# Decoder trunk on one core: the last projection and gate with tokens on partitions, two output products per feature tile in two matmuls, the first key weights in single tiles, and another table of steps

## The chip, the core and the metric

One core of a Trainium2 chip runs the whole program in one launch. The metric is the device time of one execution in microseconds (us), lower is better. TensorE (PE in the profile) multiplies matrices out of SBUF into PSUM, whose space is eight banks of 128 partitions by 512 float32; VectorE (DVE) and ScalarE (ACT) do the elementwise work; GpSimd (POOL) does a few small powers; SyncE (SP) issues nearly all DMAs.

## What is computed

Two layers on a residual stream `x` of 256 tokens by 1024 features, float32. The first mixes tokens by block-sparse attention (with 256 tokens: plain causal attention), the second by three gated branches (compressed, selected and sliding-window attention). After each mixer a per-layer embedding `p` is projected, gated and added:

```python
for i in range(DEPTH):                                  # DEPTH = 2
    h = rms_norm(x, norm_gain[i])
    x = x + (moba_layer if i % 2 == 0 else nsa_layer)(h, ...)     # q, k, v, z = h @ w_in; attention; silu(z); @ w_out
    gate = jax.nn.sigmoid(rms_norm(x, ple_gate_gain[i]) @ ple_w_gate[i])
    x = x + gate * (p[i] @ ple_w_proj[i])
return x                                                # (1, 256, 1024)
```

Here `w_out` and `ple_w_gate` are 1024 by 1024, and `ple_w_proj` is 256 by 1024.

## The kernel before

**Layout.** `x` lies in SBUF as `xT`, features on partitions: eight tiles ("k" 0 to 7) of 128 features by 256 tokens. Every float32 product is made of float32r ones: an operand is split into a high part (rounded by ACT) and a low part (the remainder, by DVE), and high x high, high x low and low x high are added in PSUM. Of a weight the parts are `hi` and `lo` (cut from `raw` or, when small, from a `tmp` buffer, where the DMA put it); of an activation they are `ah` and `al`, two tiles of 128x256. There are five `raw`, five `hi` and five `lo` buffers, and five `tmp`.

**Units.** A projection of 512 output features is a `Unit` (line 510). `mul` (529) makes its products for one k. With `feat` the features come out on partitions: the weights are stationary and the 256 tokens stream, so a tile of 128 output features takes three products of 256 columns. Without `feat` the tokens come out on partitions: an activation tile of 128 tokens is stationary and 512 weight columns stream, three products of 512 columns for each half of the tokens. q, k and v are of the second sort; z, `w_out` (steps `o0`, `o1`, in layer 1 `no0`, `no1`), the projection of `p` (`p0`, `np0`, ...) and the gate (`g0`, `ng0`, ...) of the first.

**The end of a layer** is `tail` (693). Step `x.k` gates an attention tile and splits it, `o` multiplies by `w_out`, `o>j` adds the result to `xT` (`add_out`, 723), `y.k` splits `xT` times a gain, `b` makes the norm: squares of `xT` summed in `sqacc`, two small products with `ones` into a `tr` bank, a power on POOL, two transposes that spread the result, `bc`. `g` multiplies, and `gate` (729) multiplies by `bc`, takes a tanh on ACT, multiplies by the projected `p` and adds to `xT`. In the last layer the output is stored from `xT`, feature-major, and the host transposes it.

**What sets the order.** Each step only records its operations. `PROGRAM` (line 25) is a table of steps whose order says which operation goes first when several are ready; a planner (`schedule`, 258) with costs of its own puts all operations of all engines into one order from it, and assigns the buffers. The table was found by a search. The first weights of q (`c0` to `c7`) are loaded as single tiles of one k, those of k (`k.0` to `k.3`) as pairs.

**Banks.** PSUM has the tags `mm` (four banks), `s` (two, scores) and `tr` (two, transposes and attention outputs). One line of the program (L394) issues every instruction, so the profile is read by tile names.

Of the kernel before, what the change touches and what calls it, by code (L numbers as in the profile page):

```python
# [24 lines left out]
PROGRAM = ("x0 w:c0 x2 c0 x1 w:c1 c1 x3 w:c2 c2 x4 w:c3 w:c4 x5 c3 w:c5 w:k.0 x6 w:c6 consts x7 k.0 w:c7 c4 w:k.1 c5 "  # L25
# [22 lines left out]

BEHIND = "k.0 k.2"
# [366 lines left out]
def trunk(ctx: ExitStack, tc: tile.TileContext, a, out):  # L416
# [79 lines left out]
    def split_act(src, gain=None, either=False):  # L496
        hi = apool.tile([P, T], F32R, tag="ah", name="ah")
        lo = apool.tile([P, T], F32R, tag="al", name="al")
# [9 lines left out]
        return hi, lo  # L508

    class Unit:  # L510
# [4 lines left out]
        def __init__(self, src, feat, xs, n=512, nk=KT, kg=2, apart=False, close=None):  # L515
            self.src, self.feat, self.xs, self.n, self.nk, self.kg, self.apart = src, feat, xs, n, nk, kg, apart
            self.ps, self.w, self.granules = None, {}, nk // kg
            self.whole = self.granules if close is None else close
            self.parts = [] if close is None else \
                [(b, (m,)) for b in range(2) for m in range(2)] if apart else [(0, (0, 1)), (1, (0, 1))]  # L520

        def weights(self, g):
            if self.ps is None:
                self.ps = [bank("mm", 4) for _ in range(2)]
                if self.apart:
# [3 lines left out]
        def mul(self, w, j, k, b, ms=(0, 1), cols=None, parts=(0, 1, 2)):  # L529
            (wh, wl), (xh, xl) = w, self.xs[k]  # L530
            first, last = k == 0, k == self.nk - 1
            if self.feat:
# [160 lines left out]
    def tail(i, oT, pvs, zin, xz, norm, after):  # L693
# [35 lines left out]
        def gate(u, j, m, n):  # L729
# [704 lines left out]
```

## Time and profile before

| | us |
|---|---|
| time, median of 3 runs | 361.81 (361.71 to 362.15) |
| time of the profiled execution | 362.87 |
| span of that execution, first to last instruction | 361.1 |
| TensorE busy in it | 354.9 (98%), 2569 matmul records |
| VectorE busy | 324.3 (90%) |
| ScalarE busy | 270.7 (75%) |
| main DMA queue, share of the 16 engines' span | 46.8% |

The profiled execution is 1.06 us above the median, and 1.8 us of it lie outside the span. The share of busy time of TensorE is the union of matmul records whose ends are modelled; successive matmuls overlap in them, so how fast it really goes is seen in the distance between starts. A name such as `mm<-ah,hi` is output, then inputs; the shape behind it is the moving operand's.

### The profile page before, as it was taken

The numbers are of one execution on the slowest core, as the hardware profiler recorded it, in microseconds if no ns is written. First come the engines' busy times: TensorE is split into PE (matmuls) and PEld (weight loads), VectorE is DVE, ScalarE is ACT, GpSimd is POOL, SyncE is SP. The second block draws the span as 40 slices with busy tenths as digits, with TensorE's granted clock in tenths as the row PEclk, the third lists the DMA queues.
The fourth block names the chain that finished last, engine by engine and source line by source line (L and its number), as shares of the span: only waits on it lengthen the run. The fifth ranks groups of instructions, "written<-read, shape, count | busy, mean of one in ns | idle before, by whom it ended". The sixth has DMA issues, their size and how long they took to land.

```text
span 361.1 us, 7132 instructions
## 1 busy us (share of the span) xinstructions
PE 354.9 (98%) x2569; PEld 322.3 (89%) x2569; DVE 324.3 (90%) x799; ACT 270.7 (75%) x592; POOL 29.0 (8%) x26
## 2 busy tenths in 40 slices
PE   8999999999999999999999999999999999999994
PEld 7688888888999999999889999767998999999994
DVE  5899999999999975969999999989999999967965
ACT  5667599986999854947665699969978989956711
POOL 1024104210000000000003300003000000000010
PEclk9999999999999999999999999999999999999998
DMA  7988456533554352745643534177363342142102
GB/s 223 364 315 273 160 195 230 176 118 99 178 190 148 114 181 74 227 165 176 204 136 115 211 120 172 60 285 287 129 246 134 120 130 104 57 157 80 59 31 87
DMA packets 20051, 58.97 MB, mean 163 GB/s; under 512 B 2480, under 2 KB 5296, under 8 KB 20016
## 3 DMA queue, kind: packets, MB, share of 16 engines
q1 hardware_dynamic: 19440, 58.04, 46.8%
q10 hardware_dynamic: 576, 0.48, 0.4%
q8 instruction: 20, 0.33, 0.4%
q14 instruction: 15, 0.12, 0.1%
HBM read 57.46 MB, written 1.05 MB: 162 GB/s over the span
## 4 chain that ended last, share of the span: by engine, by line
PE 92%; DVE 3%; ACT 2%; DMA 2%; issue 1%; SPq 0%; DVEq 0%; ACTq 0%
PE mm L394 71%; PE tr L394 12%; PE s L394 9%; DMA tmp<-in_p 2%; DVE lo L394 1%; DVE sm L394 1%; DVE tmp L394 1%; ACT sm L394 0%; ACT pt L394 0%; ACT tmp L394 0%; ACT hl L394 0%; ACT hi L394 0%; DVE c L394 0%; ACT big L394 0%; DVE kcB L394 0%
## 5 line engine op out<-in xcount | busy, mean ns | idle before, releaser
L394 ACT ACTIVATE hi<-raw 128x1024 fp32r<-128x1024 f32 (+2 forms) x100 | 99.0, 1006 | 29.9 <-PE mm L394 21.9
L394 DVE TENSOR_TENSOR lo<-raw,hi 128x1024 fp32r<-128x1024 f32 (+2 forms) x100 | 115.1, 1159 | 5.9 <-ACT hi L394 5.0
L394 PE MATMUL mm<-al,hi 128*128 128x256 f32 x416 | 116.9, 287 | 0.0
L394 PE MATMUL mm<-ah,lo 128*128 128x256 f32 x416 | 114.5, 286 | 0.0
L394 PE MATMUL mm<-ah,hi 128*128 128x256 f32 x416 | 114.2, 286 | 0.0
L394 PEld LDWEIGHTS mm<-al,hi 128*128 128x128 f32 x416 | 79.3, 191 | 0.2
L394 PEld LDWEIGHTS mm<-ah,lo 128*128 128x128 f32 x416 | 78.0, 191 | 0.3
L394 PEld LDWEIGHTS mm<-ah,hi 128*128 128x128 f32 x416 | 77.8, 191 | 0.4 <-issue 0.2
L394 PE MATMUL mm<-hi,ah 128*128 128x512 f32 (+2 forms) x178 | 67.5, 384 | 0.3 <-ACT hi L394 0.3
L394 PE MATMUL mm<-hi,al 128*128 128x512 f32 (+2 forms) x178 | 66.6, 377 | 0.0
L394 PE MATMUL mm<-lo,ah 128*128 128x512 f32 (+2 forms) x178 | 64.0, 377 | 0.0
L394 ACT ACTIVATE sm<-sm,nb 128x128 f32<-128x128 f32 (+1 forms) x96 | 42.6, 446 | 6.6 <-DVE nb L394 6.4
L394 PEld LDWEIGHTS mm<-hi,ah 128*128 128x128 f32 x178 | 33.9, 192 | 6.9 <-ACT hi L394 1.7
L394 PEld LDWEIGHTS mm<-hi,al 128*128 128x128 f32 x178 | 34.0, 192 | 5.1
L394 PEld LDWEIGHTS mm<-lo,ah 128*128 128x128 f32 x178 | 33.6, 191 | 5.2
L394 DVE CUSTOM_DVE_ANT_0 sm<-s,cst,nr_q 128x128 f32<-128x128 f32 (+1 forms) x96 | 36.2, 409 | 1.6 <-PE s L394 1.3
L394 ACT ACTIVATE pt<-tr 128x384 f32<-128x384 f32 x48 | 21.6, 482 | 3.9 <-PE tr L394 3.6
L394 PE MATMUL tr<-cst,sm 128*128 128x128 f32 x144 | 23.9, 274 | 0.2 <-ACT big L394 0.2
L394 POOL TENSOR_TENSOR r_q<-r,neg_half 128x16 f32<-128x16 f32 x5 | 15.8, 3150 | 77.0 <-DVE r L394 77.0
L394 ACT ACTIVATE tmp<-tmp 128x512 f32<-128x512 f32 (+3 forms) x22 | 11.2, 517 | 13.6 <-DVE tmp L394 13.5
L394 PEld LDWEIGHTS tr<-cst,sm 128*128 128x128 f32 x144 | 17.1, 140 | 2.3 <-DVE q L394 0.4
L394 ACT ACTIVATE ah<-xT,gain_in 128x256 fp32r<-128x256 f32 x31 | 14.8, 500 | 5.2 <-DVE xT L394 3.7
(176 smaller groups left out, 535.3 us busy)
## 6 DMA issues: line engine op xcount, KB each, us to landing
raw<-in_moba_in SPq DMA_DIRECT2D x28, 512.0 KB, 4.3
raw<-in_nsa_in SPq DMA_DIRECT2D x24, 512.0 KB, 3.5
raw<-in_w_out SPq DMA_DIRECT2D x16, 512.0 KB, 3.5
raw<-in_ple_gate SPq DMA_DIRECT2D x16, 512.0 KB, 3.9
raw<-in_w SPq DMA_DIRECT2D x8, 512.0 KB, 4.2
raw<-in_ple_proj SPq DMA_DIRECT2D x4, 512.0 KB, 3.8
raw<-in_nsa_vs SPq DMA_DIRECT2D x4, 304.0 KB, 2.8
xT<-in_x SPq DMA_DIRECT2D x8, 128.0 KB, 3.6
```

The lines of the kernel that those rows point to most:

```text
L394: getattr(getattr(self.nc, o.engine), o.method)(*[real(x) for x in o.args], **{k: real(x) for k, x in o.kwargs.items()})
```

## The change

1. **Fused pairs.** `split_act` puts both parts of an activation side by side in one tile of 128x512 (`both`; its names in built rows begin with `a_`). Where a unit is `wide`, each feature tile gets a PSUM bank of its own, and `mul` makes two products for it and a k instead of three: high weight by 512 columns (high and low activations at once, into the two halves of the bank) and low weight by 256 columns into the first half. The halves are added when they are taken out. `wide` are `w_out` of layer 1 (`no`) and the gate of layer 0 (`g`); half 0 of each takes all four `mm` banks, half 1 both `s` and both `tr`.
2. **Tokens on partitions** in the projection of `p` and the gate of layer 1. The gate then needs the norm as a number per partition (`rms`), which `square_x` takes on ACT from four transposed tiles at a time, and `xT` itself transposed: `turn_x` makes 16 transposes into `s` and `tr` banks. `gate_tok` runs tanh straight from PSUM with the norm as its scale, multiplies, adds and stores; the two norm products, the two transposes for `bc` and the multiplications by `bc` are gone from this layer. The output is stored token-major. The last part of the gate has 256 columns, and its end is done in two pieces of 128.
3. **Single key tiles.** The first four k of the keys' weights come as single tiles (`w:d0` to `w:d3`, products `d0` to `d3`) through `tmp` buffers.
4. **Another table `PROGRAM`**, so that most instructions stand elsewhere.

```diff
-PROGRAM = ("x0 w:c0 x2 c0 x1 w:c1 c1 x3 w:c2 c2 x4 w:c3 w:c4 x5 c3 w:c5 w:k.0 x6 w:c6 consts x7 k.0 w:c7 c4 w:k.1 c5 "
+PROGRAM = ("x0 w:c0 x1 w:c1 c0 w:d1 d0 x2 w:c2 x4 w:d2 x7 d1 x5 d2 x3 w:c3 w:d3 w:c4 w:c5 x6 consts a.1 a.3 w:c6 "
...
+WIDE = ('no', 'g')
+LAST = 1
+STORES = 4
...
     def split_act(src, gain=None, either=False):
-        hi = apool.tile([P, T], F32R, tag="ah", name="ah")
-        lo = apool.tile([P, T], F32R, tag="al", name="al")
+        both = apool.tile([P, 2 * T], F32R, tag="a2", name="a2")
+        hi, lo = both[:, :T], both[:, T:]
...
-        return hi, lo
+        return hi, lo, both
...
+            if self.wide:
+                for m in ms:
+                    o, s = self.ps[2 * b + m], slice((2 * b + m) * P, (2 * b + m + 1) * P)
+                    steps = [(o, wh[:, j, s], both)]
+                    steps.insert(0 if last else 1, (o[:, :T], wl[:, j, s], xh))
+                    for i, (d, y, x) in enumerate(steps):
+                        nc.tensor.matmul(d, y, x, start=first and i == 0, stop=last and i == len(steps) - 1,
+                                         skip_group_check=True)
+            elif self.feat:
...
+    MM, OTHER = (("mm", 4),) * 4, (("s", 2),) * 2 + (("tr", 2),) * 2
...
+        def add_out(u, j, m):
+            if u.wide:
+                for part in (slice(0, T), slice(T, 2 * T)):
+                    nc.vector.tensor_tensor(xT[:, m], xT[:, m], u.ps[j][:, part], op=OP.add)
...
+            if u.wide:
+                nc.scalar.activation(gr[:, 0], ps[:, T:], AF.Copy)
+                nc.vector.tensor_tensor(gr[:, 0], gr[:, 0], ps[:, :T], op=OP.add)
+                ps = gr.rearrange("p a b -> p (a b)")
...
+        def turn_x(h, t):
+            xps[h, t] = bank(*(("tr", 2) if h else ("s", 2)))
+            for k in range(4):
+                nc.tensor.transpose(xps[h, t][:, k * P:k * P + P], xT[:, 4 * h + k, t * P:t * P + P], ident)
...
+        def square_x(h, t):
+            nc.scalar.activation(tmp("sq"), xps[h, t], AF.Square, accum_out=sums[:, h, t:t + 1])
...
+        def gate_tok(u, j, h):
...
+                nc.scalar.activation(th, u.ps[t][:, a:b], AF.Tanh, scale=rms[:, t:t + 1])
+                nc.vector.scalar_tensor_tensor(y, th, 1.0, y, op0=OP.add, op1=OP.mult)
+                nc.vector.tensor_tensor(y, y, xps[h, t][:, a:b], op=OP.add)
...
-            u = Unit(a["ple_proj"][i, h], True, px, nk=2).steps(f"{n}p{h}")
+            u = Unit(a["ple_proj"][i, h], i == 0, px, nk=2).steps(f"{n}p{h}")
...
+                u = Unit(a["ple_gate"][i, h], False, xg, close=LAST if h else 2)
+                if h:
+                    u.parts = [(0, {}), (1, dict(cols=(0, 256))), (1, dict(cols=(256, 512)))]
```

Where instructions move. TensorE right after the products of k 1 for q (banks `mm_78`, `mm_79` are q's two halves of the tokens, in the new rows `mm_80` and `mm_81` are the keys'). Before:

```order
L394 MATMUL mm_79<-lo_130,ah_107 128x512
L394 MATMUL mm_78<-hi_126,ah_106 128x512
L394 MATMUL mm_78<-hi_126,al_115 128x512
L394 MATMUL mm_79<-hi_126,ah_106 128x512
L394 MATMUL mm_79<-hi_126,al_115 128x512
L394 MATMUL mm_78<-lo_131,ah_106 128x512
```

With the change:

```order
L399 MATMUL mm_79<-lo_125,a_1_110 128x512
L399 MATMUL mm_80<-hi_122,a_0_109 128x512 x2
L399 MATMUL mm_81<-hi_122,a_0_109 128x512 x2
L399 MATMUL mm_80<-lo_127,a_0_109 128x512
L399 MATMUL mm_81<-lo_127,a_0_109 128x512
L399 MATMUL mm_80<-hi_121,a_1_110 128x512 x2
L399 MATMUL mm_80<-lo_126,a_1_110 128x512
L399 MATMUL mm_81<-hi_121,a_1_110 128x512 x2
L399 MATMUL mm_81<-lo_126,a_1_110 128x512
L399 MATMUL mm_78<-hi_118,a_2_111 128x512 x2
```

Twelve key products on the first two x tiles now stand between q's second and third tile.

VectorE in layer 1, from the last piece of attention (`pcL`) to the first additions of `w_out` (`xT<-xT,mm`); `big<-big` gates the last attention tiles. Before:

```order
L394 TENSOR_TENSOR pcL_99<-tr_75,pcT_196 64x256
L394 TENSOR_TENSOR lo_131<-raw_136,hi_126 128x1024
L394 TENSOR_TENSOR lo_128<-raw_133,hi_123 128x1024
L394 SCALAR_TENSOR_TENSOR big_90<-big_89,big_90 128x256 x2
L394 TENSOR_TENSOR al_119<-big_90,ah_110 128x256
L394 TENSOR_TENSOR al_122<-big_90,ah_106 128x256
L394 TENSOR_TENSOR xT_63<-xT_63,mm_79 128x512
L394 TENSOR_TENSOR xT_63<-xT_63,mm_80 128x512
```

With the change:

```order
L399 TENSOR_TENSOR lo_124<-raw_128,hi_118 128x1024
L399 TENSOR_TENSOR lo_123<-raw_129,hi_120 128x1024
L399 TENSOR_TENSOR pcL_99<-tr_76,pcT_187 64x256
L399 TENSOR_TENSOR lo_127<-raw_130,hi_122 128x1024
L399 SCALAR_TENSOR_TENSOR big_88<-big_89,tr_75 128x512
L399 TENSOR_TENSOR a_5_114<-big_88,a_5_114 128x256
L399 TENSOR_TENSOR a_3_112<-big_88,a_3_112 128x256
L399 TENSOR_TENSOR xT_63<-xT_63,mm_80 128x256
L399 TENSOR_TENSOR lo_125<-raw_131,hi_119 128x1024
L399 TENSOR_TENSOR xT_63<-xT_63,mm_78 128x256
L399 TENSOR_TENSOR xT_63<-xT_63,mm_80 128x256
```

The last tiles are gated straight out of the bank, a weight split has moved in front of the additions and one between them, and each addition takes one half of a bank.

VectorE at the end of the program. Before:

```order
L394 TENSOR_TENSOR tmp_84<-s_165,bc_144 128x256
L394 TENSOR_TENSOR xT_63<-xT_63,tmp_85 128x512
L394 SCALAR_TENSOR_TENSOR tmp_83<-tmp_83,big_88 128x256
L394 TENSOR_TENSOR xT_63<-xT_63,tmp_83 128x256
L394 TENSOR_TENSOR tmp_86<-s_166,bc_144 128x128 x2
L394 SCALAR_TENSOR_TENSOR tmp_82<-tmp_82,big_88 128x128 x2
L394 TENSOR_TENSOR xT_63<-xT_63,tmp_82 128x128 x2
```

With the change:

```order
L399 SCALAR_TENSOR_TENSOR big_90<-tmp_83,big_90 128x512
L399 TENSOR_TENSOR big_90<-big_90,tr_75 128x512
L399 SCALAR_TENSOR_TENSOR big_90<-tmp_84,big_90 128x128
L399 SCALAR_TENSOR_TENSOR big_90<-tmp_85,big_90 128x128
L399 TENSOR_TENSOR big_90<-big_90,tr_76 128x128 x2
```

The multiplications by `bc` ahead of the last tanh are gone; a whole part of 512 columns now stands just ahead of the last pieces.

## Rows read from the trace of the kernel before

**Rows 1.** The page: span, TensorE's share, the chain that ended last by engine.

```profile
span 361.1 us, 7132 instructions
PE 354.9 (98%) x2569; PEld 322.3 (89%) x2569; DVE 324.3 (90%) x799; ACT 270.7 (75%) x592; POOL 29.0 (8%) x26
...
PE 92%; DVE 3%; ACT 2%; DMA 2%; issue 1%; SPq 0%; DVEq 0%; ACTq 0%
```

**Rows 2.** Timeline, TensorE: start us, us, instruction; 512 columns, then 256 columns.

```profile
20.25 0.39 PE L394 MATMUL mm<-lo,ah 128*128 128x512 f32 x1
...
21.39 0.39 PE L394 MATMUL mm<-hi,ah 128*128 128x512 f32 x1
...
344.24 0.28 PE L394 MATMUL mm<-ah,hi 128*128 128x256 f32 x1
...
345.80 0.28 PE L394 MATMUL mm<-al,hi 128*128 128x256 f32 x1
```

**Rows 3.** TensorE's timeline: norm products, transposes; one product left out of each.

```profile
341.76 0.50 PE L394 MATMUL tr<-ones,sqacc 128*128 128x2 f32 x4
...
342.32 0.28 PE L394 MATMUL mm<-ah,lo 128*128 128x256 f32 x1
...
346.52 0.38 PE L394 MATMUL tr<-cst,rstd 128*128 128x128 f32 x2
...
346.86 0.29 PE L394 MATMUL mm<-ah,lo 128*128 128x256 f32 x1
```

**Rows 4.** Timeline, TensorE (PEld: weight loads): a block of attention-times-value products.

```profile
320.47 0.28 PE L394 MATMUL mm<-ah,lo 128*128 128x256 f32 x1
...
320.68 2.82 PE L394 MATMUL tr<-pt,v 128*64 128x256 f32 x32
...
323.43 0.19 PEld L394 LDWEIGHTS tr<-pcT,vcB 128*128 128x128 f32 x1 [0.17 <-issue]
```

**Rows 5.** Busy by stretch (PE, PEld, DVE, ACT, ...); timelines at the start.

```profile
7.00:17.00 10.00, 9.73 (x39) 6.78 (x39) 8.48 (x16) 7.58 (x15) 0.00 (x0) 1.00 0.97 333
...
8.35 0.39 PE L394 MATMUL mm<-hi,ah 128*128 128x512 f32 x1
...
10.32 0.63 ACT L394 ACTIVATE hi<-raw 128x512 fp32r<-128x512 f32 x1 [1.25 <-DMA raw<-in_moba_in]
11.57 0.51 ACT L394 ACTIVATE ah<-xT,gain_in 128x256 fp32r<-128x256 f32 x1 [0.62 <-DMA xT<-in_x]
```

**Rows 6.** VectorE around layer 1's `w_out`; a group (busy, mean ns | idle).

```profile
321.54 2.36 DVE L394 TENSOR_TENSOR lo<-raw,hi 128x1024 fp32r<-128x1024 f32 x2 [1.82 <-ACT hi L394]
324.84 0.76 DVE L394 SCALAR_TENSOR_TENSOR big<-big,big 128x256 f32<-128x256 f32 x2 [0.94 <-ACT big L394]
...
328.28 0.69 DVE L394 TENSOR_TENSOR xT<-xT,mm 128x512 f32<-128x512 f32 x1 [1.77 <-PE mm L394]
329.48 0.69 DVE L394 TENSOR_TENSOR xT<-xT,mm 128x512 f32<-128x512 f32 x1 [0.51 <-PE mm L394]
...
L394 DVE TENSOR_TENSOR xT<-xT,tmp 128x256 f32<-128x256 f32 x7 | 2.8, 419 | 0.0
```

**Rows 7.** The end: timelines of three engines, a group of ScalarE.

```profile
356.22 0.28 PE L394 MATMUL s<-ah,lo 128*128 128x256 f32 x1
...
356.54 0.49 DVE L394 TENSOR_TENSOR tmp<-s,bc 128x128 f32<-128x128 f32 x2 [0.21 <-PE s L394]
...
356.92 0.51 ACT L394 ACTIVATE tmp<-tmp 128x128 f32<-128x128 f32 x2 [1.51 <-DVE tmp L394]
...
357.26 0.49 DVE L394 SCALAR_TENSOR_TENSOR tmp<-tmp,big 128x128 f32<-128x128 f32 x2 [0.24 <-ACT tmp L394]
357.67 0.49 DVE L394 TENSOR_TENSOR xT<-xT,tmp 128x128 f32<-128x128 f32 x2
...
358.19 0.36 ACTq L394 DMA_DIRECT2D out<-xT  x1
...
L394 ACT ACTIVATE v<-mm,rstd 128x256 f32<-128x256 f32 x4 | 1.8, 473 | 0.0
```

More of the change, by code (lines that the diff above doesn't have):

```diff
@@ L518, in __init__ @@
             self.whole = self.granules if close is None else close
             self.parts = [] if close is None else \
-                [(b, (m,)) for b in range(2) for m in range(2)] if apart else [(0, (0, 1)), (1, (0, 1))]
+                [(b, dict(ms=(m,))) for b in range(2) for m in range(2)] if apart else [(0, {}), (1, {})]
         def weights(self, g):
             if self.ps is None:
-                self.ps = [bank("mm", 4) for _ in range(2)]
-                if self.apart:
+                self.ps = [bank(*b) for b in self.wide or (("mm", 4),) * 2]
@@ L526, in weights, with mul @@
+                if self.apart and not self.wide:
                     self.ps = [ps[:, :T] for ps in self.ps + [bank("s", 2) for _ in range(2)]]
             self.w[g] = split(self.src[g], (self.kg, self.n))
-        def mul(self, w, j, k, b, ms=(0, 1), cols=None, parts=(0, 1, 2)):
-            (wh, wl), (xh, xl) = w, self.xs[k]
+        def mul(self, w, j, k, b, ms=(0, 1), cols=None, parts=(0, 1, 2), only=False):
+            (wh, wl), (xh, xl, both) = w, self.xs[k]
             first, last = k == 0, k == self.nk - 1
-            if self.feat:
+            if self.wide:
[7 more added lines that the diff above has]
+            elif self.feat:
@@ L541, in mul @@
                 c0, c1 = cols or (0, self.n)
+                w0, w1 = (c0, c1) if only else (0, c1 - c0)
                 o, s = self.ps[b][:, c0:c1], slice(b * P, b * P + P)
@@ L544, in mul @@
                     x, y = ((xh, wh), (xl, wh), (xh, wl))[i]
-                    nc.tensor.matmul(o, x[:, s], y[:, j], start=first and c0 == i == 0, stop=last and i == 2,
+                    nc.tensor.matmul(o, x[:, s], y[:, j, w0:w1], start=first and c0 == i == 0, stop=last and i == 2,
                                      skip_group_check=True)
@@ L746, in gate @@
-            if not last:
-                for k in range(m, m + n):
-                    after(k)
+            if u.wide:
+                nc.scalar.activation(gr[:, 0], ps[:, T:], AF.Copy)
+                nc.vector.tensor_tensor(gr[:, 0], gr[:, 0], ps[:, :T], op=OP.add)
+                ps = gr.rearrange("p a b -> p (a b)")
+            nc.vector.tensor_tensor(gr, ps.rearrange("p (a b) -> p a b", a=n),
+                                    n1.bc[:, None, :].to_broadcast([P, n, T]), op=OP.mult)
@@ new lines, in gate_tok @@
+        def gate_tok(u, j, h):
+            t, only = u.parts[j]
+            c0, c1 = only.get("cols") or (0, 512)
+            last = h == 1 and j == len(u.parts) - 1
+            for a, b in ((c0, c0 + P), (c0 + P, c1)) if last else ((c0, c1),):
+                th, y = tmp("th")[:, :b - a], pt[:, t, 512 * h + a:512 * h + b]
+                nc.scalar.activation(th, u.ps[t][:, a:b], AF.Tanh, scale=rms[:, t:t + 1])
+                nc.vector.scalar_tensor_tensor(y, th, 1.0, y, op0=OP.add, op1=OP.mult)
+                nc.vector.tensor_tensor(y, y, xps[h, t][:, a:b], op=OP.add)
+                for c in range(a, b, 512 // STORES if not h else 512):
+                    d = min(b, c + 512 // STORES) if not h else b
+                    (nc.scalar if last and a > c0 else nc.sync).dma_start(
+                        out[t, :, 512 * h + c:512 * h + d], pt[:, t, 512 * h + c:512 * h + d])
@@ L769, in tail @@
             todo[f"{n}y.{k}"] = lambda k=k: split_g(k)
-        n1.steps(f"{n}b")
+        if i:
+            todo[f"{n}b"] = norm_x
+        else:
+            n1.steps(f"{n}b")
     def pairs_pv(o, pairs):
@@ L810, in trunk @@
         o.after.append(i)
-    pair = [None]
+    pair = {}
     lows = {}
@@ L825, in first_w @@
             return
+        low = lows[k]
         c0, raw = 512 * (k % 2), second if k == 1 else None
         if k >= 4:
-            if not c0:
-                pair[0] = wpool.tile([P, 1024], F32, tag="raw", name="raw", bufs=NRAW)
-            raw = pair[0][:, c0:c0 + 512]
+            if k // 2 not in pair:
+                pair[k // 2] = wpool.tile([P, 1024], F32, tag="raw", name="raw", bufs=NRAW)
+            raw = pair[k // 2][:, c0:c0 + 512]
             nc.sync.dma_start(raw, a["moba_in"][0, k // 2, :, c0:c0 + 512])
@@ L860, in __init__ @@
                       "q": Unit(a["moba_in"][1], False, x0).steps("1q") if h else uq0}
+            if not h:
+                u = self.u["k"]
+                for k in range(4):
+                    todo[f"w:d{k}"], todo[f"d{k}"] = (lambda k=k: self.single(u, k)), (lambda k=k: self.tile(u, k))
+                for g in range(2):
+                    del todo[f"w:k.{g}"], todo[f"k.{g}"]
             for step in ("qe", "ke", "q", "k", "v"):
@@ L863, in __init__, with single, tile @@
             todo[n + "q+"], todo[n + "k+"] = (lambda: self.q2()), (lambda: self.k2())
+        def single(self, u, k):
+            if u.ps is None:
+                u.ps = [bank("mm", 4) for _ in range(2)]
+            u.w[f"d{k}"] = split(a["moba_in"][2, k // 2, :, 512 * (k % 2):512 * (k % 2) + 512], (1, 512), small=True)
+        def tile(self, u, k):
+            for b in range(2):
+                u.mul(u.w[f"d{k}"], 0, k, b)
         def qe(self):
@@ L985, in trunk @@
         todo[f"next.{k}"] = lambda k=k: next_x(k)
-    tail(0, oT, pvs, [a["moba_in"][6 + h] for h in range(2)], x0, n0, lambda k: None)
+    tail(0, oT, pvs, [a["moba_in"][6 + h] for h in range(2)], x0, n0)
     pe = consts.tile([P, 2, 16], F32, name="pe")
@@ L1314, in trunk @@
                 KD0=lambda: KD(0), KD1=lambda: KD(1))
-    tail(1, oT, pvs1, [a["nsa_in"][4 + h] for h in range(2)], x1, n2, lambda k: nc.sync.dma_start(out[:, k], xT[:, k]))
+    tail(1, oT, pvs1, [a["nsa_in"][4 + h] for h in range(2)], x1, n2)
     def run(step):
@@ L1432 @@
     got = r.results[0]["out_0"]
-    return _np.ascontiguousarray(got.transpose(1, 0, 2).reshape(D, T).T)[None]
+    return _np.ascontiguousarray(got.reshape(T, D))[None]
```

76 lines of the change are left out of this document (44 added, 32 removed), and 43 rows, old and new, of the table PROGRAM.

## The prediction

> **What bounds the kernel now.** First the page: of a span of 361.1 us TensorE is busy for 354.9, and the chain that ended last is TensorE for 92% [rows 1]. So the time is what TensorE needs for its list of products, plus the few places where it waits, plus the end behind its last product. How long it needs is not the mean of a matmul record, since records overlap: it is the distance between starts. In the timeline five steps of 512-column products take 1.14 us, 0.228 each, and thirteen steps of 256 columns take 1.56, 0.120 each [rows 2]. Twice 0.120 is more than 0.228: a product costs its columns and about 13 ns besides (0.240 less 0.228, by a step of 0.427 ns a column). That small difference is what most of the change lives on, for it leaves the number of columns as it is.
>
> TensorE waits in few places. Between 7 and 17 us it makes 39 products of 512 columns, 8.9 us of work in 10 [rows 5]; behind that the records leave next to nothing open. Its last product starts at 356.22, and the span ends 4.9 us later [rows 1, 7]. VectorE is busy 90% [rows 1], close to being the next bound, so each edit is also weighed there.
>
> **Fused pairs and tokens on partitions.** Counted in the built programs, products of 256 columns go from 1484 to 1024, those of 512 from 458 to 688. It comes out by hand: 128 pairs of a feature tile and a k are fused (64 each in `w_out` of layer 1 and the gate of layer 0), and of the three 256s of each two become one 512, -256 and +128 in all; the projection of `p` and the gate of layer 1 give up 48 + 192 of 256 for 102 of 512 and 36 of 256 (the last part is cut in two). Together -460 and +230, the same columns. By the paces: 460 x 0.120 = 55.2 less 230 x 0.228 = 52.4, so **-2.8 us**, all of it on the path, since TensorE is the path.
>
> The Trainium skill ("TensorE: Matmul & The Clock Gate", section "Wait — 56ns, not 53.3ns?") gives a warm matmul about 2.5 ns beyond its columns. By that figure the sum would lose most of this term: an estimate from it is 230 x 2.5 ns = 0.6 us. The rows disagree, with 13 ns a product, and they decide.
>
> **Added to TensorE.** 16 transposes of `xT`, less the two that spread the norm. Two transposes with one 256-column product among them take 0.34 us from 346.52 to 346.86 [rows 3], so 0.11 each: 14 x 0.11 = **+1.5 us**. The norm products of layer 1 go: four records with one product among them take 0.56, less 0.12 [rows 3]: **-0.4 us**. The new order has nine blocks of attention-value or compression products with a half-filled array, one more than before; a block costs its entry (0.21 to the next start for 0.12) and the 0.17 at its exit [rows 4], together 0.26: **+0.3 us**. TensorE in all: -2.8 + 1.5 - 0.4 + 0.3 = -1.4.
>
> **The start.** TensorE loses 10 - 39 x 0.228 = 1.1 us there, because weights and x tiles arrive late: the split at 10.32 had waited 1.25 us for its DMA, and that at 11.57 0.62 [rows 5]. With the change the keys' products `d0` and `d1` need only the first two x tiles and stand behind `c1`: 12 more products, 2.7 us, from about 8.35, where the third tile of q begins now [rows 5], to 11.1. Then `c2` is wanted. In SP's new order six x tiles and five weight tiles lead up to it, 6 x 128 + 5 x 256 = 2048 KB. The x split that waited until 11.57 had the same 2048 KB ahead of it and with it (x tiles 0 to 5 in its order of loading, `c0` to `c4`). So at worst `c2` is there at 11.5 and split at 12.1 (0.63 for a hi half [rows 5]): a wait of 1.0, and nothing gained. At best it comes earlier, as the transfers behind that x tile no longer share the engines, and all 1.1 goes. I take the middle, **-0.5**, bounds -1.1 and 0.
>
> **The join from attention to `w_out` of layer 1.** This is where VectorE gets more. Four additions of 512 (0.69 each) become 16 of 256 (0.42 each) [rows 6]: 6.7 - 2.8 = +3.9 us, and one weight split (2.36 for two) moves in front of the additions: +1.2. Against it, VectorE idles there for 1.82 + 0.94 + 1.77 + 0.51 = 5.0 us [rows 6]. So it goes from idle to just full. What hides it: between the first product on the last attention tile and the first gate product on tile 7 of the eight, TensorE has 22 products of 512, 24 of 256, then 16 transposes and 45 of 512, 67 x 0.228 + 24 x 0.12 + 16 x 0.11 = 19.9 us. VectorE owes in that time 16 additions (6.7), eight splits (0.48, 3.8 in all) and some five weight splits (1.2, 6.0): 16.5. It is covered, with 3.4 us to spare in sum, less at single places. I cost it at 0. If the cover fails: only the 1.77 + 0.51 of idle lies between additions, where more of them can go, so 5.1 - 2.3 = 2.8 is the most that TensorE could wait. The straight gating out of the bank (one operation of 512 in place of a copy and two of 256) shortens the same chain a little; I leave it out.
>
> **The gate of layer 0** gets a copy on ACT and an addition on VectorE for each of eight tiles, 8 x 0.42 = 3.4 us. Behind its last product the new order has 49 products of 512 of the next layer, 11.2 us, before the last x tile is used, and the chain of one tile is about nine operations of 0.4 to 0.5: hidden, 0. Without cover it would be one copy and one addition, 0.8.
>
> **The end.** Now: last product 356.22, multiplication by `bc` at 356.54, tanh at 356.92, two more operations, store issued at 358.19 [rows 7]. With the change tanh starts where the multiplication did; a tanh of 128 columns from PSUM with a scale is bounded by 0.47 for 256 [rows 7] and by the 0.3 that the present ones take apart. The first hop of 0.38 goes, up to 0.2 comes back in two slower tanhs: **-0.25**, bounds -0.5 and +0.1 (a part of 512 columns is finished just ahead on VectorE, and may be late).
>
> **Sum**: -1.4 - 0.5 - 0.25 = -2.15. The profiled execution took 362.87, so 360.7 for one like it; against the median, 361.81 - 2.15 = **359.7 us**.
>
> **The rivals.**
> *More waits go.* The whole 1.1 at the start (another -0.6), the end at -0.5, the extra block free (-0.3): 358.5. For it: all are bounds from rows. Against it: c2's 2048 KB.
> *The join turns into a wait.* VectorE comes late to the additions of `w_out`, the transposes of `xT` and the splits for the gate wait for it, and TensorE for them. Half of the 2.8 gives 361.1, about level with before. All of it, with nothing gained at the start, gives 359.7 + 2.8 + 0.5 = 363.0, **slower than before**. It decides at a wait of 2.1 us. For it: VectorE full where it idled. Against it: 3.4 us to spare.
> *The pairs don't do what they say.* Weights have to be loaded for each product; if in a 512 + 256 pair that shows, and a pair costs as three 256s, the 2.8 is gone: 359.7 + 2.8 = 362.5. For it: mixed runs of the two widths are few in the trace. Against it: 256-column products, each with a load of its own, keep 0.12. With the 0.6 that the skill's figure leaves (2.5 ns a product), it would be 361.9; as a mechanism here it means that the 0.12 is held up by something other than the product, and the even thirteen steps [rows 2] speak against it.
>
> **How the numbers follow.** Chances: forecast 0.55, more waits go 0.17, the join at half 0.11, the join in full 0.10, the pairs 0.05, the 2.5 ns 0.02. A measurement of this kernel tells about 0.2% from no change, 0.7 us: faster is below 361.1, slower above 362.5. Faster takes the forecast, the first rival and half of the join at half: 0.77; the rest of that, the 2.5 ns and half of the pairs are the same: 0.11; slower 0.12. The forecast's own range is 358.9 to 360.6 (start and end at their bounds, the join's first 0.3). The range over the cases, 358.0 to 361.9, leaves out some 0.06 below and 0.13 above.
>
> **What would show it.** Between steady starts 0.228 and 0.120 in the fused runs; last product near 354 in the span; one gap of up to 1 us on TensorE near 11 to 12 us, ended by ACT or VectorE's split of `c2`, and none behind it; at the end tanh directly behind the last product. Wrong would be: a wait of TensorE on VectorE between the last attention block and the gate of layer 1; pairs at over 0.36; or gaps in stretches that I have not looked at, since nearly every instruction moves.

## The result, and the profile after

The changed kernel takes 364.43 us (364.25 to 365.1, six runs); the kernel before, beside it, 361.98 (361.54 to 362.9, six runs). The ratio is 1.0072, 95% interval 1.0059 to 1.0086: **slower by 2.45 us**, where 2.15 less had been forecast. The profiled execution of after took 364.85, that of before 362.87.

The page of after (busy us, share of the span, instructions; then the chain that ended last by engine and by line) answers to [rows 1]:

```profile
span 362.7 us, 6746 instructions
...
PE 355.0 (98%) x2349; PEld 311.6 (86%) x2349; DVE 324.2 (89%) x806; ACT 274.4 (76%) x607; POOL 26.1 (7%) x26
...
PE 91%; DMA 5%; DVE 3%; ACT 1%; issue 0%; ACTq 0%; DVEq 0%
```

TensorE has 220 records less than before, and VectorE is no busier. But in the chain the share of DMA went from 2% to 5%. It is the first thing to follow. What TensorE waited for in after (us in total, times, longest):

```profile
PE mm L399 <- DVE hi L399: 1.4, 1, 1.4
PE tr L399 <- DVE ones L399: 1.1, 1, 1.1
PE s L399 <- DVE hl L399: 0.8, 1, 0.8
PE mm L399 <- ACT hi L399: 0.3, 1, 0.3
PE s L399 <- DVE nb L399: 0.2, 1, 0.2
```

and in before:

```profile
PE tr L394 <- DVE ones L394: 1.1, 1, 1.1
PE mm L394 <- ACT hi L394: 0.3, 1, 0.3
PE tr L394 <- ACT big L394: 0.2, 1, 0.2
```

The 1.1 at `ones` is the program's first microsecond and stands in both. New are 1.4, 0.8 and 0.2: two places stand out, and neither wait is at a product that was edited. A start delayed by a wait loses more than the idle shown here (1.5 for the 1.4, 0.9 for the 0.8, by the distance between starts), since the record ahead of it is drawn to its modelled end.

**The start** answers to [rows 5]. SyncE's issues and what hung on them in after (start, us, engine, instruction; in brackets the idle before it and what ended it):

```profile
1.63 0.43 SPq L399 DMA_DIRECT2D xT<-in_x  x1
2.10 0.91 SPq L399 DMA_DIRECT2D tmp<-in_moba_in  x2
...
6.96 0.51 ACT L399 ACTIVATE a<-xT,gain_in 128x256 fp32r<-128x256 f32 x1 [2.56 <-DMA xT<-in_x]
...
8.28 1.16 PE L399 MATMUL mm<-hi,a 128*128 128x512 f32 x4 [1.37 <-DVE hi L399]
...
15.73 0.50 PE L399 MATMUL mm<-hi,a 128*128 128x512 f32 x1 [0.25 <-ACT hi L399]
...
7.00:17.00 10.00, 8.47 (x36) 6.45 (x36) 8.21 (x16) 7.03 (x14) 0.00 (x0) 1.00 0.94 298
```

The chain (start, us, what) begins with the load of `c1`, issued by ACT:

```profile
1.66 6.02 DMA tmp<-in_moba_in
```

TensorE stands between `c0` and `c1` for 1.37 us; in the stretch from 7 to 17 (length, then busy time of PE, PEld, DVE, ACT and POOL, granted clock, DMA share, GB/s) it makes 36 products of 512 instead of 39. The wait at 11 to 12 that the prediction spoke of did not come, though a smaller one stands at 15.73. What was late was `c1` itself, which landed at 7.68 (5.39 in before), and the second x tile to be loaded, whose split begins at 6.96. In before:

```profile
1.64 1.37 SPq L394 DMA_DIRECT2D xT<-in_x  x3
...
5.23 1.46 ACT L394 ACTIVATE ah<-xT,gain_in 128x256 fp32r<-128x256 f32 x3 [0.74 <-DMA xT<-in_x]
```

There the second x tile was issued at the same time, 1.64, and split 1.7 us earlier. Behind it stood two more x tiles of 128 KB; in the new order two key weights of 256 KB stand there (issued at 2.10 and 2.57), the first of the single tiles.

**The third quarter.** Two stretches, columns as above, in before:

```profile
220.00:240.00 20.00, 20.00 (x126) 15.57 (x125) 18.74 (x58) 16.11 (x47) 0.00 (x0) 1.00 0.38 133
240.00:260.00 20.00, 19.95 (x166) 16.40 (x165) 19.03 (x68) 19.56 (x56) 3.15 (x2) 1.00 0.70 260
```

and in after:

```profile
220.00:240.00 20.00, 19.82 (x130) 17.17 (x129) 19.62 (x68) 19.12 (x61) 0.00 (x0) 1.00 0.14 51
240.00:260.00 20.00, 19.73 (x172) 15.46 (x168) 18.16 (x57) 17.52 (x49) 3.16 (x2) 1.00 0.85 290
```

The new order moves little data from 220 to 240 (51 GB/s for 133) and more behind it (290 for 260). The place where that shows, from after's chain (start, us, what) and its timelines:

```profile
251.47 5.53 DMA raw<-in_nsa_in
...
257.02 1.06 ACT L399 ACTIVATE hi<-raw 128x1024 fp32r<-128x1024 f32 x1 [1.12 <-DMA raw<-in_nsa_in]
258.11 1.23 DVE L399 TENSOR_TENSOR lo<-raw,hi 128x1024 fp32r<-128x1024 f32 x1 [1.35 <-ACT hi L399]
259.77 1.41 DVE L399 TENSOR_TENSOR hl<-tr,hl 64x512 fp32r<-64x512 f32 x2
260.51 0.50 PE L399 MATMUL s<-v_1r,hl 128*128 128x256 f32 x2 [0.78 <-DVE hl L399]
```

Weights of `z` in layer 1, issued at 251.47, take 5.53 us. ACT waits for them with the split, VectorE stands behind ACT with the low half, and the subtraction that makes the low half of the selected queries, `hl`, comes behind that in VectorE's order. It has nothing to do with these weights, but the scores wait for it, and TensorE for them.

**The steps of the sum.** The fused pairs in a steady run (256s ahead of them, from 148.24), and the gate with tokens on partitions; these answer to [rows 2]:

```profile
148.24 0.40 PE L399 MATMUL mm<-a,hi 128*128 128x256 f32 x2
...
149.32 0.40 PE L399 MATMUL mm<-a,hi 128*128 128x512 f32 x1
...
151.79 0.40 PE L399 MATMUL mm<-a,hi 128*128 128x512 f32 x1
...
345.41 0.62 PE L399 MATMUL mm<-hi,a 128*128 128x512 f32 x2
...
349.49 0.62 PE L399 MATMUL mm<-hi,a 128*128 128x512 f32 x2
```

Nine products of 256 columns take 1.08 us from 148.24 to 149.32, 0.120 each. The seven pairs that follow take 2.47, 0.353 each; three 256s would be 0.360 and a 512 and a 256 by the paces of the prediction 0.348. Eighteen 512s in a row take 4.08, 0.2267 each.

The transposes of `xT`, answering to [rows 3], four at a time: 0.36 us for the first, 0.44 and 0.35 for the next two, so 16 cost 1.4 to 1.5.

```profile
340.65 0.60 PE L399 MATMUL tr<-cst,xT 128*128 128x128 f32 x4
341.01 0.70 PE L399 MATMUL mm<-hi,a 128*128 128x512 f32 x2
...
343.84 0.60 PE L399 MATMUL s<-cst,xT 128*128 128x128 f32 x4
344.28 0.60 PE L399 MATMUL tr<-cst,xT 128*128 128x128 f32 x4
344.63 0.48 PE L399 MATMUL mm<-hi,a 128*128 128x512 f32 x1
```

The half-filled array, answering to [rows 4]: two blocks of 16 products in layer 0, at 110.80 and 112.62, where before has one of 32 at 84.6. A few scores' products stand between them; each block pays its own entry and exit, 0.09 and 0.15 over the paces in nearly all of them.

```profile
110.80 1.52 PE L399 MATMUL tr<-pt,v 128*64 128x256 f32 x16
...
112.62 1.52 PE L399 MATMUL tr<-pt,v 128*64 128x256 f32 x16
```

The join, answering to [rows 6]: the stretch of `w_out` of layer 1 has no wait of TensorE, with VectorE at 15.58 of 20.

```profile
320.00:340.00 20.00, 20.00 (x129) 16.85 (x128) 15.58 (x33) 11.52 (x19) 0.00 (x0) 1.00 0.50 166
```

The end, answering to [rows 7], and the DMA of the stretch from 360 to 366 in after:

```profile
358.46 0.28 PE L399 MATMUL mm<-lo,a 128*128 128x256 f32 x1
358.84 0.63 ACT L399 ACTIVATE tmp<-mm,rstd 128x128 f32<-128x128 f32 x2 [1.46 <-PE mm L399]
359.24 0.55 DVE L399 SCALAR_TENSOR_TENSOR big<-tmp,big 128x128 f32<-128x128 f32 x2 [0.34 <-ACT tmp L399]
...
360.22 0.36 ACTq L399 DMA_DIRECT2D out<-big  x1
...
q14 instruction: 1, 0.01, 0.4%
```

Tanh follows the last product directly. From that product to the end of the span it is 362.7 - 358.46 = 4.2 us, before 361.1 - 356.22 = 4.9: 0.6 less. But 364.85 - 362.7 = 2.15 lie outside the span, before 362.87 - 361.1 = 1.77. In that 0.4 falls one 8 KB fetch of instructions, at 364.31, behind everything the program does. All ten executions of this kernel here have 2.1 to 2.2 us outside the span, those of every other kernel here 1.7 to 1.9.

### The profile page after: what moved, and what is told of

Read it like the earlier page. It is cut to its first block, busy times and chain, and to the rows that moved or that the text cites. A ratio compares the mean times of both kernels' runs of the same rounds, so it can differ in the third digit from the quotient of the medians.

```text
span 362.7 us, 6746 instructions
## 1 busy us (share of the span) xinstructions
PE 355.0 (98%) x2349; PEld 311.6 (86%) x2349; DVE 324.2 (89%) x806; ACT 274.4 (76%) x607; POOL 26.1 (7%) x26
## 4 chain that ended last, share of the span: by engine, by line
PE 91%; DMA 5%; DVE 3%; ACT 1%; issue 0%; ACTq 0%; DVEq 0%
PE mm L399 66%; PE tr L399 15%; PE s L399 9%; DMA tmp<-in_moba_in 3%; DMA raw<-in_nsa_in 2%; DVE sm L399 1%; DVE lo L399 1%; ACT hi L399 0%; DVE kd_0r L399 0%; DVE v_1r L399 0%; ACTq L399 0%; DVE big L399 0%; DVE hl L399 0%; ACT tmp L399 0%; DVE a L399 0%
## 5 line engine op out<-in xcount | busy, mean ns | idle before, releaser
L399 PE MATMUL mm<-hi,a 128*128 128x512 f32 (+2 forms) x448 | 129.7, 377 | 1.7 <-DVE hi L399 1.4
L399 PE MATMUL mm<-a,hi 128*128 128x256 f32 (+1 forms) x544 | 112.9, 300 | 0.0
L399 PEld LDWEIGHTS mm<-hi,a 128*128 128x128 f32 x448 | 80.1, 191 | 15.9 <-ACT a L399 1.6
L399 PEld LDWEIGHTS mm<-a,hi 128*128 128x128 f32 x544 | 86.1, 190 | 3.0 <-issue 0.3
L399 PE MATMUL mm<-a,lo 128*128 128x256 f32 x304 | 82.0, 286 | 0.0
L399 PE MATMUL mm<-lo,a 128*128 128x512 f32 (+2 forms) x224 | 81.0, 372 | 0.0
L399 PEld LDWEIGHTS mm<-a,lo 128*128 128x128 f32 x304 | 56.7, 190 | 1.5 <-DVE lo L399 0.3
L399 PEld LDWEIGHTS mm<-lo,a 128*128 128x128 f32 x224 | 42.0, 190 | 6.8 <-DVE lo L399 0.2
L399 PE MATMUL tr<-cst,sm 128*128 128x128 f32 x144 | 23.3, 275 | 0.0
L399 ACT ACTIVATION_READ_ACCUMULATOR sm<-sm,nb 128x1 f32 x96 | 18.2, 190 | 0.0
L399 DVE TENSOR_SCALAR sm<-sm,l 128x128 f32<-128x128 f32 (+1 forms) x64 | 17.4, 314 | 0.1
```

The source lines that it names most:

```text
L399: getattr(getattr(self.nc, o.engine), o.method)(*[real(x) for x in o.args], **{k: real(x) for k, x in o.kwargs.items()})
```

## The experiments

A number used for all: the **time over pace**. From the trace each distance between two starts on TensorE is taken, less what that product takes in a steady run (0.2267 for 512 columns, 0.120 for 256, 0.109 for a transpose of 128 columns, and so on), and summed over a stretch. It holds waits, entries and exits of the half-filled array, and small surcharges where kinds of products change. The program's first 1.1 us are left out of it; the expectations below count them, so their 4.8 is 3.7 here.

| us over pace, stretch | before | before again | after | after again | e1 | e2 | e5 | e6 |
|---|---|---|---|---|---|---|---|---|
| 0 to 20 | 3.0 | 1.5 | 3.7 | 2.6 | 2.5 | 2.5 | 1.9 | 1.4 |
| 20 to 100 | 1.0 | 1.0 | 0.9 | 0.9 | 1.2 | 0.9 | 1.2 | 1.0 |
| 100 to 120 | 0.0 | 0.0 | 1.2 | 1.3 | 0.4 | 1.3 | 0.4 | 0.0 |
| 120 to 220 | 0.7 | 0.7 | 1.0 | 1.0 | 1.0 | 1.0 | 1.0 | 0.7 |
| 220 to 240 | 0.7 | 0.8 | 1.3 | 1.3 | 1.4 | 1.3 | 1.5 | 0.8 |
| 240 to 260 | 0.9 | 1.0 | 1.7 | 1.9 | 1.1 | 0.7 | 1.1 | 1.3 |
| 260 to 300 | 1.2 | 0.8 | 1.2 | 1.1 | 1.1 | 1.5 | 1.5 | 1.7 |
| 300 to the end | 0.3 | 0.4 | 1.1 | 1.1 | 0.9 | 1.5 | 1.5 | 0.7 |
| in all | 7.8 | 6.2 | 12.0 | 11.2 | 9.6 | 10.5 | 10.1 | 7.4 |

The start differs most from execution to execution of one kernel; the other rows repeat within 0.4.

**Both kernels again**, each with a second profile.

> The kernel before once more, to have its trace from the same chip as the experiments. Both theories: 361.7 (361.2 to 362.3); TensorE's time over its pace in 0 to 20 us 4.0 as in the first trace, or, if the chip sets it, 3.5.

> The changed kernel once more on the same chip as the experiments. Theory A (waits of the new order, their size set by when loads land): 364.0 (363.5 to 364.6); with a start like the experiments' (3.5 us over pace in 0 to 20 us instead of 4.8) a longer gap at 2S2 near 258 us, 1.8 to 2.4 us instead of 0.94. Theory B (the start's 1.65 us gap is fixed by the order of its loads and is the loss): the same start as in the first trace, 4.8 over pace, and 364.4.

Before: 361.79 us; after: 364.65 (363.99 to 365.0), ratio to the runs of before on that chip 1.0075 (1.0054 to 1.0097). The result repeats. Neither expectation for after held: the start fell, as A had it, to 2.6 in the table, but the wait at `hl` stayed at 1.0 where A had 1.8 to 2.4, and the median lies just above A's range. The start of before fell too, to 1.5, below both sizes expected. The two profiled executions, 361.21 and 363.99, differ by 2.78, and their traces give the ledger used below: the products at their paces -2.0, time over pace +5.0 (the pairs and the products with tokens on partitions cost some 0.5 each more than those paces, which lies in it), last product to end of span -0.6, outside the span +0.4 (again with an 8 KB instruction fetch 1.6 us behind the span, which no trace of another kernel here has).

**e1: the old first third.** The steps of before up to position 119 of the table (some 95 us), then the rest of after's table; the keys' first weights in pairs, as this order has them.

```diff
-PROGRAM = ("x0 w:c0 x1 w:c1 c0 w:d1 d0 x2 w:c2 x4 w:d2 x7 d1 x5 d2 x3 w:c3 w:d3 w:c4 w:c5 x6 consts a.1 a.3 w:c6 "
+PROGRAM = ("x0 w:c0 x2 c0 x1 w:c1 c1 x3 w:c2 c2 x4 w:c3 w:c4 x5 c3 w:c5 w:k.0 x6 w:c6 consts x7 k.0 w:c7 c4 w:k.1 c5 "
...
-BEHIND = "d0 k.2"
+BEHIND = "k.0 k.2"
```

> The changed kernel with the table's steps of before up to the second half's first scores (about the first 95 us), keys' weights as pairs again; the rest of the table, the fused pairs and the tokens on partitions as changed. Theory A (the new order puts waits in, the edits themselves do what was forecast): the 1.65 us between the last product of c0 and the first of c1 goes, as do the waits of the new order up to 110 us; TensorE's lag over its planned starts falls from 2.4 us at 20 us to about 1.0, and the time from 364.4 to 363.0 (362.6 to 363.6). Theory B (the edits in the two tails cost what the table shows as lost, the start only moves time): 364.4, less than 0.4 off the changed kernel.

362.38 us (361.99 to 364.52), ratio to before 1.0026 (1.0011 to 1.0041): 1.7 of the lost 2.5 us come back with the order of the first third, a little more than theory A had. Of these, 0.4 lie outside the span, where e1 has 1.8 as before has. In the table the rest is at 100 to 120 (1.2 to 0.4: one block of 32 products again) and at 240 to 260. The last was not foreseen: that stretch's steps are after's, but buffers and loads stand otherwise, and the wait at `hl` is 0.2 here, in one trace of a load that scatters by more (table under e2). At the start the gain is not shown: 2.5 lies close to the 2.6 of after again, and the gap before `c1` that theory A would take away still stands in this trace:

```profile
7.33 1.25 PE L399 MATMUL mm<-hi,a 128*128 128x512 f32 x4 [1.38 <-ACT a L399]
```

Here it ends with the split of the third x tile, which `c1` needs in this order. It landed at 6.74, in the other four traces of the old order at 5.76 to 6.02.

**e2: a later load in the plan.** The planner is told that the load which came at 257.00 lands 2 us later than it reckons, so it puts work that doesn't need it in front.

```diff
+LATE = {'w:nz0.3': 2000.0}
...
+                t += LATE.get(o.step, 0.0)
```

> The changed kernel, where the planner is told that one load, the last weights of layer 1's z (nz0.3), lands 2 us later than its model says; so the split of that load stands further back on ACT and VectorE, and nothing else is edited. Theory A (this late load is what holds the scores 2S2 up at 259 us, 0.94 us): that gap of TensorE goes, some of it comes back in the changed order behind, 363.9 (363.5 to 364.2). Theory B (the gap has another cause, the load only stands beside it): the gap stays at 0.9 or moves, 364.4 (364.1 to 364.8).

363.31 us, ratio to before 1.0049 (1.0028 to 1.0069). The timelines of ACT, VectorE and TensorE in e2 at this place:

```profile
256.78 1.41 DVE L403 TENSOR_TENSOR hl<-tr,hl 64x512 fp32r<-64x512 f32 x2
257.02 1.05 ACT L403 ACTIVATE hi<-raw 128x1024 fp32r<-128x1024 f32 x1
257.81 0.54 PEld L403 LDWEIGHTS s<-v_1r,hl 128*128 128x128 f32 x4
```

The split comes at the same time as in after, 257.02, but the subtraction stands ahead of it, and TensorE goes on: over pace 0.7 us in that stretch for 1.7 and 1.9. The load itself is no faster, 5.76 us for 5.53. This shows the mechanism, as an order on VectorE behind a load. Part of it is given back in the next two rows of the table, 260 to the end (3.0 for 2.2 and 2.3). By the ratios e2 is 0.9 us better than after, with intervals that overlap, and 0.4 of that lie outside the span.

Five traces have the subtraction behind this load's split, and in them TensorE's wait follows the load one for one:

| us | e1 | after | after again | e4 | e3 |
|---|---|---|---|---|---|
| load of these weights, issue to landing | 4.98 | 5.53 | 5.73 | 6.45 | 6.98 |
| idle of TensorE at `hl` | 0.22 | 0.78 | 0.97 | 1.68 | 2.22 |

The difference is 4.75 to 4.77 in all five. In e2 and e5, with the subtraction in front, loads of 5.76 and 7.47 us bring no wait there.

**e3: no pairs in `w_out` of layer 1.**

```diff
-WIDE = ('no', 'g')
+WIDE = ('g',)
```

> The changed kernel with w_out of layer 1 in three products of 256 columns again (64 pairs less), two banks a half as before; everything else as changed. Theory A (a fused pair saves the 13 ns of the forecast): 64 x 13 ns = 0.85 us slower, 365.3 (364.8 to 365.8). Theory B (pairs save nothing, or the two additions a tile hold TensorE at the join from attention): as fast or faster, 363.6 to 364.4.

365.13 us (364.68 to 366.2), ratio to before 1.0096 (1.0075 to 1.0116). TensorE's waits, the longest:

```profile
PE s L398 <- DVE hl L398: 2.2, 1, 2.2
```

The wait at `hl`, which lies ahead of the edit, was 2.2 us in this execution, so the time says little on the pairs by itself: **inconclusive**. The trace does say something. All 192 products of `w_out` of layer 1, with what they cost where kinds change, take 24.0 us here and 23.9 in before; the 128 of after take 23.3. The 64 pairs save 0.6 to 0.7 us.

**e4: the last projection and gate with features on partitions**, as in before (norm products, multiplication by `bc`, feature-major output); the rest is after's.

```diff
-            u = Unit(a["ple_proj"][i, h], i == 0, px, nk=2).steps(f"{n}p{h}")
+            u = Unit(a["ple_proj"][i, h], True, px, nk=2).steps(f"{n}p{h}")
...
-                u = Unit(a["ple_gate"][i, h], False, xg, close=LAST if h else 2)
```

> The changed kernel with the projection of p and the gate of layer 1 with features on partitions again (norm by ones products, bc, feature-major output), the order otherwise as changed. Theory A: TensorE's list there is 0.3 us longer (240 x 0.120 + 0.4 + 2 transposes against 102 x 0.228 + 36 x 0.120 + 16 transposes), the end 0.25 to 0.6 later: 365.1 (364.7 to 365.8). Theory B (tokens on partitions cost more than the forecast had, by waits for the transposes or for the late parts): 363.4 to 364.3.

365.36 us (364.4 to 365.67), ratio 1.0093 (1.0075 to 1.0112). Worse than after by the ratios, 0.7 us; but the same wait stands ahead here too, 1.7 us, and the 0.4 outside the span is missing. It fits a gain from this part of the change and does not measure it.

**e5: e1 and e2 together.**

```diff
+LATE = {'w:nz0.3': 2000.0}
...
-BEHIND = "d0 k.2"
+BEHIND = "k.0 k.2"
```

> The steps of before up to the first scores' end as in e1_old_start, and the late landing of nz0.3 told to the planner as in e2_late_nz03. Theory A: the two gains are of the same gap in part (e1 moved the loads, and had 0.38 us left at 2S2), so 0.4 under e1: 362.0 (361.6 to 362.5), level with before; what is left of the forecast's 2 us is then lost in many small waits. Theory B (each of the two is worth its own gain): 361.3 or less.

362.18 us (361.65 to 362.77), ratio 1.0003 (0.999 to 1.0015): level with before. The two don't add up, as theory A had it: in e1's trace 0.2 was left of the wait that e2 takes.

**e6: before's order up to the middle of layer 1's attention**, then after's rest. It keeps the pairs in `w_out` of layer 1 and the tokens on partitions; pairs in the gate of layer 0 and single key tiles, which before's order has no place for, are left out.

```diff
-WIDE = ('no', 'g')
+WIDE = ('no',)
...
-BEHIND = "d0 k.2"
+BEHIND = "k.0 k.2"
```

> Steps of before up to the first third of layer 1's attention (about 250 us of the program), then the rest of the table of after; edits kept: w_out of layer 1 in fused pairs, the last projection and gate with tokens on partitions. Left out of the edits: pairs in the gate of layer 0, single key tiles. All of the computation stays. Theory (the edits save about what the lists say and only the new order of the first 260 us loses it): 64 pairs save 64 x 0.007 to 0.012 = 0.4 to 0.8, tokens 1.4, ones 0.4, transposes cost 1.5, the end gives 0.3 to 0.6, sum -1.0 to -1.7, and the waits of the first 260 us are those of before: 360.1 to 360.9, faster than before, first loads landing as in before and DMA share of 220 to 240 near 0.4. Rival (the edits themselves bring waits in the tail, or the late loads are a matter of the last third's order too): 361.8 or more. Waits in 300 to the end then above 1 us over pace.

360.98 us (360.69 to 362.24, 12 runs) beside 361.68 of before (17 runs), ratio 0.9983 (0.9972 to 0.9993): **faster than both kernels**, by 0.7 us. That is just short of what the first theory gave (360.1 to 360.9) and 0.8 from the rival's 361.8. The page of e6, its stretches, and a row each of its start and end:

```profile
span 359.0 us, 6817 instructions
...
220.00:240.00 20.00, 20.00 (x122) 15.42 (x121) 18.43 (x62) 16.12 (x48) 0.00 (x0) 1.00 0.41 144
240.00:260.00 20.00, 19.87 (x169) 16.43 (x168) 19.09 (x62) 19.31 (x56) 3.16 (x2) 1.00 0.64 228
...
5.17 0.51 ACT L399 ACTIVATE a<-xT,gain_in 128x256 fp32r<-128x256 f32 x1 [0.46 <-DMA xT<-in_x]
...
354.68 0.28 PE L399 MATMUL mm<-lo,a 128*128 128x256 f32 x1
```

The second x tile is split at 5.17, the DMA share is 0.41 where after has 0.14, and up to 240 us nothing is lost against before. So the edits that e6 keeps don't bring the waits; the new order does, together with the single key tiles, which stand at its head and which no run tried apart from it. Not all of the gain arrives, though: from 240 to 300 e6 loses 2.9 us over pace, as after does (2.9 and 3.0), where before loses 1.8 and 2.1. No single gap in it is above 0.3. Profile against profile (360.80 and 361.21 in all), the products at their paces give -1.1 and the end -0.5 (359.0 - 354.68 = 4.3, for 4.8), and the time over pace takes 1.2 back.

**e7 and e8: what stands behind the second x tile.** Before's table with one load moved (in the changed kernel's code with its edits off; the two parts of an activation still share a tile): in e7 the 256 KB of `c2` right behind the second x tile, in e8 a pair of key weights, 512 KB in one transfer.

```diff
-PROGRAM = ("x0 w:c0 x2 c0 x1 w:c1 c1 x3 w:c2 c2 x4 w:c3 w:c4 x5 c3 w:c5 w:k.0 x6 w:c6 consts x7 k.0 w:c7 c4 w:k.1 c5 "
+PROGRAM = ("x0 w:c0 x2 w:c2 c0 x1 w:c1 c1 x3 c2 x4 w:c3 w:c4 x5 c3 w:c5 w:k.0 x6 w:c6 consts x7 k.0 w:c7 c4 w:k.1 c5 "
```

```diff
+PROGRAM = ("x0 w:c0 x2 w:k.0 c0 x1 w:c1 c1 x3 w:c2 c2 x4 w:c3 w:c4 x5 c3 w:c5 x6 w:c6 consts x7 k.0 w:c7 c4 w:k.1 c5 "
```

> The kernel before with one step moved: the load of c2 (256 KB) is issued right behind the second x tile instead of two x tiles (128 KB each) later. All of the computation stays. Theory (a transfer issued right behind a small one shares the engines with it and so delays it, in proportion to its size): the second x tile, issued near 1.64, lands between 5.4 and 6.3 (4 traces with x tiles behind it 5.1 to 5.3; 5 traces with two 256 KB loads 6.5 to 6.9). Rival (the late landing has to do with something else of the new order): 5.1 to 5.4.

> The kernel before with one step moved: the load of the first pair of key weights (512 KB) is issued right behind the second x tile. The keys' products are not moved up, so later loads stand worse and the whole time is not to be compared. All of the computation stays. Theory (transfers issued right behind a small one delay it by sharing the engines): the second x tile, issued near 1.64, lands at 6.4 to 6.9, as in the five traces of the new order, which have as many bytes behind it. Rival: 5.1 to 5.4, as in the other traces of the old order.

The split of that tile on ACT, in e7, then in e8:

```profile
6.28 0.51 ACT L399 ACTIVATE a<-xT,gain_in 128x256 fp32r<-128x256 f32 x1 [1.76 <-DMA xT<-in_x]
```

```profile
5.92 0.51 ACT L399 ACTIVATE a<-xT,gain_in 128x256 fp32r<-128x256 f32 x1 [1.46 <-DMA xT<-in_x]
```

The tile lands at 6.19 in e7 and 5.83 in e8; with x tiles behind it, in five traces of the old order, at 5.08 to 5.34; with two weights of 256 KB, in five of the new, at 6.46 to 6.89. It was issued at 1.63 to 1.65 in all of them. So a transfer issued *later* on the same queue does make an earlier one late, by 0.5 to 1.8 us. That the delay goes by bytes is refuted: one transfer of 512 KB costs less than one of 256 KB. One execution each; what it does go by stays open. For `c1`, which ended TensorE's wait in after, it is less clear: it landed at 6.53 and 6.31, in the old order at 5.39 to 6.34, in the new at 6.82 to 7.68.

The times, one execution each beside 362.19 of before on that chip: e7 365.10, e8 373.57. In e8 other loads stand worse, as expected, so its time says nothing. In e7 most of the loss is one wait of TensorE, for `c1`:

```profile
8.47 1.31 PE L399 MATMUL mm<-hi,a 128*128 128x512 f32 x4 [2.46 <-ACT hi L399]
```

One load moved forward by two x tiles went with a loss as large as that of the whole change.

## Why the prediction was wrong, by its steps

The ledger is that of the two profiled executions on one chip, 2.78 apart; the forecast was -2.15.

| us | forecast | measured |
|---|---|---|
| pairs and tokens | -2.8 | -2.1 |
| transposes, less the norm's products | +1.1 | +0.9 |
| half-filled array | +0.3 | +0.45 |
| start | -0.5 | +1.1 |
| end, with what lies outside the span | -0.25 | -0.25 |
| three single waits at 109, 223 and 258 | 0 | +1.8 |
| spread, in pieces under 0.25 | 0 | about +0.9, the rest of the sum |

- **Fused pairs and tokens: right in kind, mis-sized by a quarter.** Layer 0's gate goes from 23.2 to 22.6 us and layer 1's `w_out` from 23.9 to 23.3, so the pairs save 1.2 instead of 128 x 0.012 = 1.5: a pair costs 0.353, not 0.348. The projection and gate of layer 1 go from 29.0 to 28.1, up to the last product, so tokens save 0.9; by the paces alone it would be 240 x 0.120 - 102 x 0.2267 - 36 x 0.120 = 1.4, and the rest goes where kinds of products change. The rival that pairs do nothing falls, and so does the one by the Trainium skill's figure of 2.5 ns a product ("TensorE: Matmul & The Clock Gate", section "Wait — 56ns, not 53.3ns?"): the trace has 2 x 0.120 - 0.2267, 13 ns, as in before.
- **Transposes, norm products, half-filled array: right**, all within 0.2. The 16 transposes take 1.4, and 0.5 for the norm's products and their spreading goes. One block of 32 that became two of 16 is the extra one; entries and exits of all such blocks go from 1.94 to 2.39.
- **The join: right**, no wait; nor at the gate of layer 0. The rival that was costed highest did not occur.
- **The end: right in sum, by two errors.** In the span it gave 0.6, more than twice the forecast; outside the span 0.4 came back, which no step had a term for.
- **The start: wrong, and in these two executions outside both its bounds.** The step took the bytes ahead of `c2` as the only thing that could be late, and let everything ahead of it come as in before. It costed what stands *in front* of a transfer and not what was put *behind* it: both issued as early as before, the x tile came 1.1 to 1.8 us later and `c1` 0.5 to 2.3. "None behind it" and "the wait at 11 to 12" were the tests the prediction named, and the rows refute both. Since the start scatters by 1 us or more in each kernel, the mean is the better size: five traces of the new start average 2.7 over pace, five of the old 2.1, so some +0.7 for the forecast -0.5. The two groups overlap, so that the start gained nothing is well supported, and how much it lost is not.
- **What was left out: the step that failed most.** "Behind that the records leave next to nothing open" was read off the trace of before and then used for an order in which nearly every instruction stands elsewhere. It is a fact about that order, and says nothing on which work stands behind which load in another. (The old order also spread its loads, 0.38 and 0.70 of the DMA engines in two stretches for 0.14 and 0.85. That this is why they came in time is not shown: e1, with 0.12 and 0.90, has a wait of only 0.2.) 2.7 us of the 4.9 between forecast and ledger lie here. The prediction named it at its end, as "gaps in stretches that I have not looked at", and gave it no chance and no price; all its rivals that cost time were about the edits.
- **Sums that don't come out.** If a pair cost as three 256s, only the pairs' 1.5 would be gone and not the tokens' 1.2, so that rival gives 361.2 and not 362.5. The upper end of the forecast's own range, 360.6, leaves out the 0.3 of the join that it names; with it, it is 360.9. 0.240 less 0.228 is 12 ns. None of these reaches the measured 364.43.
- **Which of it is shown.** That the order, with the single key tiles, and not the edits at the ends of the layers loses the time: e6 (faster than before with the pairs in `w_out` of layer 1, the tokens on partitions and the old order to 250 us), e1 and e5 (near before and level with it, with the pairs in both places). That the wait at 258 is an order on VectorE behind a late load: e2, e5 and the five traces above. That later transfers delay the x tile: e7, e8; for `c1` it is argued. Why that one load took 5.53 us is not shown: it lies in the burst, and one of the 16 KB instruction fetches falls into it, which is a coincidence in time and no more. The spread part, the 0.4 outside the span, and e6's loss between 240 and 300 stay open: the pieces are small, and no run took them away one by one.

## What to carry to other kernels

A trace that shows no waits shows that its own order has none; when a change moves most instructions, price the new order by itself: where loads were spread and are now bunched, which transfers now stand behind a small early one, and which unrelated work stands behind a split that waits for a load. When an edit saves a per cent or less, put it into the old order first, as in e6: there those that it keeps were worth 0.7 us, and in the new order all of them were hidden by 5 us over pace. Moving cheap, ready work in front of an operation that waits for a load took the load's scatter off the path in e2 and e5; look then at what it moves behind, since e2 gave 0.7 back there.

## What was unexpected of the hardware

- A transfer of 128 KB issued at 1.63 to 1.65 landed at 5.1 to 5.3, 5.8, 6.2 or 6.5 to 6.9 us depending on what was issued *behind* it on the same queue (128 KB tiles; one of 512 KB; one of 256 KB; two of 256 KB). The Trainium skill ("DMA: Bandwidth & Descriptors", section "Two DMAs through the same engine are not ordered") says that descriptors within one queue of one DMA engine start in order but are pipelined; that allows such a delay, and no run here shows by which path it comes.
- An instruction fetch of 8 KB 1.6 us after the end of the span stood in both traces of after, with 2.2 us outside the span, and in no other trace, where it was 1.8. The Trainium skill ("Runtime: NRT & Kernel Launch", section "Instruction fetch mechanics") calls the cost of crossing a 16 KiB boundary of instructions mostly hidden. Here 0.4 us goes with a fetch behind the last work; that the fetch is the cause was not tried.
- A 512-column product followed by 256 columns does not run at the pace of its own kind: 0.236 for the 512 and 0.117 for the 256 behind it in the steady run, 0.353 a pair, where 512s among themselves keep 0.2267.
